# Two heads of a pair in the two column halves of TensorE's array, with the scattering of the second head's rows moved to GpSimd's DMAs

## The chip, the core and the metric

The kernel runs on one core of a Trainium2 chip, in one launch. The metric is the device time of that launch in microseconds. The kernel before took 2098.72 us (median of three runs, 2098.59 to 2098.99).

## What is computed

The reference is a small encoder trunk: two layers, each with a SwiGLU feed-forward block, a mixing block, cross-attention into 256 memory tokens and a second feed-forward block, on 512 frames of 1024 channels, all in float32. The change lies in the mixing block, and there in the gated recurrence of its four heads (128 key channels each):

```python
def step(S, inp):                                # over chunks of 64 frames
    qc, kc, vc, gc = inp                         # gc: log of the gate f
    b = jnp.cumsum(gc, axis=2)
    o_inter = jnp.einsum('bhtk,bhkv->bhtv', qc * jnp.exp(b), S)
    rel = b[:, :, :, None, :] - b[:, :, None, :, :]
    decay = jnp.exp(jnp.where(causal, rel, -jnp.inf))
    A = jnp.einsum('bhtk,bhsk,bhtsk->bhts', qc, kc, decay)
    o = o_inter + jnp.einsum('bhts,bhsv->bhtv', A, vc)
    ...
```

The score of frame t against an earlier frame s is a sum over key channels of q, k and the product of all gates between s and t. The kernel uses chunks of 128 frames in place of 64, and forms the scores without exponentials, by doubling.

## The kernel before

**Layout.** Activations lie transposed, channels on the 128 partitions and 512 frames along the free axis. Most products are made as three single-precision passes of split operands (`mm3`, lines 84 to 86): the weights are cut by ScalarE (line 76) and VectorE (line 77) into a high and a low part, from raw blocks that SyncE's DMAs bring in (line 140). `Weights.next` cuts five blocks and loads seven blocks ahead. Instructions are put in order for each engine by a scheduler, so the order on an engine is near that of the program, but not the same.

**Slots.** Most of the tiles in SBUF come from one pool of 38 equal slots of 4 KB a partition (`s_tile`). A slot is reused when all readers of its tile are done, DMAs that read it among them. Short-lived tiles in PSUM come from a pool of four banks (`ps_tile`), accumulators from another four.

**Score levels.** Heads are held in pairs: `g` is the pair, `hh` the head in it. `qf[g]` and `kg[g]` (128 channels x 2 heads x 512 frames) hold queries and keys times the gates of their own block. At level m (1, 2, 4, ... 64) a block of 2m frames has a first half with keys and a second half with queries, and the scores between the halves are products of `kg` and `qf`. `levels` (line 809) is a generator that is moved on at chosen ticks (`STEPS`), in between the projections that go on at the same time: four gate projections (line 911), the value projection (line 924) and the four projections of the pooling group (line 935).

- Levels 2 to 32 are done by `dense(g, m)` (line 785). For each head and each of the four chunks it multiplies the 64 packed keys (`keys[g]`, copied by `first_halves`, lines 773 and 777) with the 64 query columns of that chunk (line 793): eight float32 products of 64 weight columns and 64 moving columns for a pair, each made by the chip as two passes. Their results, 64 x 64 each, lie side by side in partitions 0 to 63 of one PSUM bank.
- Levels 2 to 16: ScalarE copies the bank to `packed` (line 802, 64 partitions x 512, once for each pair). When both pairs are there, DMAs of ScalarE's queue (line 807) scatter its rows into `spread[m]`, a tile over 128 partitions: 2, 4, 8 and 4 DMAs at levels 2, 4, 8 and 16. One step later `place` (lines 758 to 763) writes the wanted entries into the score tile `atd[g]`, under a mask, on VectorE.
- Level 32: four small copies of ScalarE for each pair (line 798) write straight into `atd[g]`.
- Level 64: line 831, again eight float32 products of 64 x 64 columns for each pair, and one copy for each pair (line 832).
- After the products of a level VectorE multiplies the gates into `kg` (line 849) and `qf` (line 850) for the next one.

After the levels come `turn` (transposes of `kg`, line 874), `carry` (the state, lines 884 to 888) and `read` (the output, lines 974 to 985). Next to them runs the pooling group: `u` (line 939), its running sums on GpSimd (lines 938 and 942), `pt` (line 946), a small product (`pooled`, line 961). GpSimd's own DMAs before the change are adding ones: two sums of weights (line 134) and sums of squares for a norm (line 403).

Of the kernel before, what the change touches and what calls it, by code (L numbers as in the profile page):

```python
# [7 lines left out]
F32 = mybir.dt.float32  # L8
# [6 lines left out]
P = 128  # L15
D = 1024
T = 512
# [3 lines left out]
NT = T // P  # L21
# [25 lines left out]
def trunk_kernel(ctx: ExitStack, tc: tile.TileContext, ap: dict, out: bass.AP):  # L47
    nc = tc.nc
    pe, act, dve, pool = nc.tensor, nc.scalar, nc.vector, nc.gpsimd
# [11 lines left out]
    def ps_tile():  # L61
        return pp.tile([P, 512], F32, tag="ps", name="ps")
# [5 lines left out]
    def s_tile(shape, dt, name):  # L68
        return sp.tile(shape, dt, tag="s", name=name)
# [401 lines left out]
    HT = T // 2  # L471
# [242 lines left out]
    def mix(l, norm, mem, after):  # L714
# [4 lines left out]
        atd = [s_tile([P, 2, NT, P], F32, "atd") for _ in range(2)]  # L719
# [3 lines left out]
        for h in range(H):  # L723
            ps = ps_tile()
# [12 lines left out]
        for h in range(H):  # L737
            ps = ps_tile()
# [6 lines left out]
        def products(a, b):  # L745

            t = tp.tile([P, T], F32, tag="sq", name="qk", bufs=4)
            hl = s_tile([P, 2, T], F32R, "qkp")
            pool.tensor_tensor(t if len(a.shape) == 2 else t.rearrange("p (h n) -> p h n", h=2), a, b, op=ALU.mult)
            split(hl[:, 0], hl[:, 1], t)  # L750
            return hl

        def column_sums(ps, hl):

            for c in range(2):
                pe.matmul(ps, ones_r, hl[:, c], start=c == 0, stop=c == 1)  # L756

        def place(g, m, rows):

            o = atd[g].rearrange("p h i (b e j) -> p (h i) b e j", e=2, j=m)[:, :, :, 1, :]  # L760
            src = rows.rearrange("p (x b j) -> p x b j", x=2 * NT, j=m)
            mk = masks[m].rearrange("p (o b j) -> p o b j", o=1, j=m).broadcast_to([P, 2 * NT, 64 // m, m])
            dve.copy_predicated(o, mk, src)

        keys = [None, None]

        def first_halves(g, m):


            keys[g] = tp.tile([P, T], F32, tag="sq", name="keys", bufs=4)  # L770
            src = kg[g].rearrange("p h (b e j) -> p h b e j", e=2, j=m)[:, :, :, 0, :]
            if m > 4:
                act.copy(keys[g].rearrange("p (h b j) -> p h b j", h=2, j=m), src)
                return
            for hh in range(2):
                dst = keys[g][:, hh * HT:(hh + 1) * HT].rearrange("p (i j b) -> p i b j", i=NT, j=m)
                act.copy(dst, src[:, hh].rearrange("p (i b) j -> p i b j", i=NT))
# [4 lines left out]
        spread = {m: spreads[i % 2] for i, m in enumerate((2, 4, 8, 16))}  # L782
        packed = [None]

        def dense(g, m):


            ps = ps_tile()
            for hh in range(2):
                for i in range(NT):  # L790
                    c = hh * HT + i * 64
                    b = qf[g][:, hh, i * P:(i + 1) * P].rearrange("p (b e j) -> p b e j", e=2, j=m)[:, :, 1, :]
                    pe.matmul(ps[0:64, c:c + 64], keys[g][:, c:c + 64], b, start=True, stop=True)  # L793
            if m == 32:
                for b in range(2):
                    src = ps[b * 32:b * 32 + 32].rearrange("p (h i t) -> p h i t", h=2, i=NT)[:, :, :, b * 32:b * 32 + 32]
                    for hh in range(2):
                        act.copy(atd[g][b * 64:b * 64 + 32, hh, :, b * 64 + 32:b * 64 + 64], src[:, hh])
                return
            if g == 0:  # L800
                packed[0] = s_tile([64, 2, T], F32, "packed")
            act.copy(packed[0][:, g], ps[0:64])
            if g == 1:
                n = max(m, 64 // m)
                for x in range(64 // n):
                    rows = slice(x, P, 2 * m) if m <= 4 else slice(2 * m * x, 2 * m * x + m)
                    nc.scalar.dma_start(spread[m][rows], packed[0][x * n:(x + 1) * n])

        def levels():

            tot = f
            odd = [qf[g].rearrange("p h (n e) -> p h n e", e=2)[:, :, :, 1] for g in range(2)]
            even = [kg[g].rearrange("p h (n e) -> p h n e", e=2)[:, :, :, 0] for g in range(2)]
            near = [[products(q[g][:, hh], kg[g][:, hh]) for hh in range(2)] + [products(odd[g], even[g])] for g in range(2)]
            yield
            for m in (1, 2, 4, 8, 16, 32, 64):
                nb = T // (2 * m)
                tots = [None, None]  # L820
                if 1 < m <= 32:
                    for g in range(2):
                        dense(g, m)
                elif m > 32:
                    for g in range(2):
                        ps = ps_tile()
                        for hh in range(2):
                            for i in range(NT):
                                a = kg[g][:, hh, i * P:i * P + 64]
                                b = qf[g][:, hh, i * P + 64:(i + 1) * P]  # L830
                                pe.matmul(ps[0:64, (hh * NT + i) * 64:(hh * NT + i + 1) * 64], a, b, start=True, stop=True)
                        act.copy(atd[g][0:64, :, :, 64:128].rearrange("p h i t -> p (h i) t"),
                                 ps[0:64, :].rearrange("p (x t) -> p x t", t=64))
                for g in range(2):
                    if m == 1:
                        for hh in range(2):
                            ps = ps_tile()
                            column_sums(ps, near[g][hh])
                            dve.tensor_tensor(atd[g][:, hh], ps.rearrange("p (i t) -> p i t", t=P),
                                              ident.rearrange("p (o t) -> p o t", o=1).broadcast_to([P, NT, P]), op=ALU.mult)  # L840
                            yield
                        ps = ps_tile()
                        column_sums(ps, near[g][2])
                        place(g, m, ps)
                    tv = tot[g].rearrange("p h (b e) -> p h b e", e=2)
                    kv = kg[g].rearrange("p h (b e j) -> p (h b) e j", e=2, j=m)
                    qv = qf[g].rearrange("p h (b e j) -> p (h b) e j", e=2, j=m)
                    tx = tot[g].rearrange("p h (b e) -> p (h b) e", e=2)
                    dve.tensor_tensor(kv[:, :, 0, :], kv[:, :, 0, :], tx[:, :, 1:2].broadcast_to([P, 2 * nb, m]), op=ALU.mult)
                    dve.tensor_tensor(qv[:, :, 1, :], qv[:, :, 1, :], tx[:, :, 0:1].broadcast_to([P, 2 * nb, m]), op=ALU.mult)  # L850
                    nt_ = s_tile([P, 2, nb], F32, "tot") if m == 1 else sm.tile([P, 2, nb], F32, tag=f"tot{m}", name="tot", bufs=2)
                    dve.tensor_tensor(nt_, tv[:, :, :, 0], tv[:, :, :, 1], op=ALU.mult)
                    tots[g] = nt_
                    if m < 32:
                        first_halves(g, 2 * m)
                    if m == 1:
                        yield
                if 2 < m <= 32:
                    for g in range(2):
                        place(g, m // 2, spread[m // 2][:, g])  # L860
                if m > 1:
                    yield
                tot = tots
            last.extend(tot)
# [26 lines left out]
        def recurrent():  # L891
            yield from levels()
            turn(0), turn(1), turn(2)
            yield
# [14 lines left out]
        for h in range(H):  # L909
            ps = ps_tile()  # L910
# [7 lines left out]
        for k2 in range(NK // 2):  # L918
            wh, wl = wts.next()
            for e in range(2):  # L920
                k = 2 * k2 + e
                for i in range(NT):
                    sl = slice(i * P, (i + 1) * P)
                    mm3(accs[i], (norm.h[k][0][:, sl], norm.h[k][1][:, sl]), (wh[:, e], wl[:, e]),
                        start=k == 0, stop=k == NK - 1)
# [6 lines left out]
        for g in POOL_ORDER:  # L932
            win = 2 ** (g + 1)
            ps = ps_tile()
# [5 lines left out]
            src, dst, w_ = u, sa, 1  # L940
            while w_ < win:
                pool.tensor_tensor(dst[:, 16:], src[:, 16:], src[:, 16 - w_:16 + T - w_], op=ALU.add)
                src, dst = dst, (sb if dst is sa else sa)
# [23 lines left out]
        o = [None] * H  # L967
# [328 lines left out]
```

## Time and profile before

| | |
|---|---|
| median of three runs | 2098.72 us |
| the profiled execution: span | 2096.8 us |
| TensorE (PE) busy | 2087.3 us, 100% |
| VectorE (DVE) busy | 1412.3 us, 67% |
| ScalarE (ACT) busy | 919.8 us, 44% |
| GpSimd (POOL) busy | 205.0 us, 10% |
| products of levels 2 to 32 (line 793) | 320 passes |
| products of level 64 (line 831) | 64 passes |
| DMAs of line 807 | 36, on ScalarE's queue |

The page gives no total for the profiled execution beside its span. The span lies 1.9 us below the median of the runs, and that difference is taken as what lies around the span.

The profile names an instruction by engine, line, and "out<-in" tiles. PEld is the loading of weights into TensorE's array, which can go on beside a product; "128*64" is the number of rows and columns of the array that an instruction uses. "x32" is a count of instructions that were merged into one row. The time in square brackets is how long the engine stood idle before a row, and what ended that. A release that the profile can't name is "issue". Queues of an engine are written ACTq, POOLq and SPq.

### The profile page before, as it was taken

Reading aid. Unit: us, or ns where it says so; the run is one execution under the profiler, and the core shown is the slowest. Engines: PE = TensorE matmul, PEld = TensorE weight load, DVE = VectorE, ACT = ScalarE, POOL = GpSimd, SP = SyncE. Lnnn points to the kernel's source line nnn. Section 1 sums busy time; section 2 is a strip of 40 time slices with the busy share of each in tenths; the row PEclk is TensorE's granted clock in tenths of the full one; section 3 lists DMA queues with packets and bytes.
Section 4 is the critical chain, followed back from the end, with each engine's and each line's share of the span. In section 5 each row is a group of like instructions: output and inputs, shape, how many; then the busy total and the mean of one; then the engine's idle time right before and its main releaser. Section 6 shows DMA issues by size and latency. Waiting matters only on the chain.

```text
span 2096.8 us, 29543 instructions
## 1 busy us (share of the span) xinstructions
PE 2087.3 (100%) x11538; PEld 1809.1 (86%) x11538; DVE 1412.3 (67%) x2126; ACT 919.8 (44%) x1465; POOL 205.0 (10%) x204
## 2 busy tenths in 40 slices
PE   9999999999999999999999999999999999999998
PEld 8889898888888888989888898988888888889897
DVE  7758576677646585766776685757776556768575
ACT  6425344434544343544534353445344444435343
POOL 1100000302000110000021000003210001100000
PEclk9999999999999999999999999999999999999999
DMA  5364554233533246646425746532334331474552
GB/s 187 119 182 124 145 156 161 61 99 98 151 103 103 61 131 171 157 122 185 123 69 153 188 116 177 158 108 71 92 112 135 111 112 45 141 208 124 146 138 79
DMA packets 107868, 268.33 MB, mean 128 GB/s; under 512 B 10832, under 2 KB 12880, under 8 KB 107728
## 3 DMA queue, kind: packets, MB, share of 16 engines
q1 hardware_dynamic: 93952, 224.49, 32.9%
q0 software_dynamic: 11952, 38.02, 10.3%
q10 hardware_dynamic: 1824, 3.93, 0.8%
q8 instruction: 91, 1.49, 0.3%
q14 instruction: 49, 0.40, 0.1%
HBM read 256.70 MB, written 2.10 MB: 123 GB/s over the span
## 4 chain that ended last, share of the span: by engine, by line
PE 98%; DVE 1%; issue 1%; ACT 0%; POOL 0%; POOLq 0%; ACTq 0%; DVEq 0%
PE ps L86 19%; PE ps L84 19%; PE ps L85 19%; PE acc L554 8%; PE acc L84 8%; PE acc L85 8%; PE acc L86 8%; PE acc L555 4%; PE ps L1025 1%; PE ps L793 1%; PE ps L1026 1%; PE ps L974 0%; PE ps L1091 0%; PE acc L346 0%; PE ps L756 0%
## 5 line engine op out<-in xcount | busy, mean ns | idle before, releaser
L77 DVE TENSOR_TENSOR wlo<-raw,whi 128x1024 fp32r<-128x1024 f32 (+1 forms) x334 | 394.5, 1202 | 78.4 <-ACT whi L76 63.2
L76 ACT CAST whi<-raw 128x1024 fp32r<-128x1024 f32 (+1 forms) x334 | 330.3, 1018 | 113.1 <-DMA raw<-in_ffn_w_dram 49.9
L85 PE MATMUL ps<-h,whi 128*128 128x512 f32 x848 | 330.2, 390 | 0.0
L84 PE MATMUL ps<-h,whi 128*128 128x512 f32 x848 | 329.7, 391 | 0.0
L86 PE MATMUL ps<-h,wlo 128*128 128x512 f32 x848 | 329.5, 390 | 0.0
L554 PE MATMUL acc<-bhl,whi 128*128 128x512 f32 x744 | 266.3, 398 | 0.0
L86 PE MATMUL ps<-bhl,wlo 128*128 128x256 f32 x744 | 210.8, 284 | 0.2
L85 PE MATMUL ps<-bhl,whi 128*128 128x256 f32 x744 | 209.9, 283 | 0.0
L84 PE MATMUL ps<-bhl,whi 128*128 128x256 f32 x744 | 209.8, 283 | 0.0
L555 PE MATMUL acc<-bhl,wlo 128*128 128x256 f32 x744 | 204.8, 281 | 0.0
L76 ACT CAST whi<-wsum 128x1024 fp32r<-128x1024 f32 x124 | 130.1, 1050 | 151.8 <-DVE wsum L165 87.3
L86 PEld LDWEIGHTS ps<-h,wlo 128*128 128x128 f32 x848 | 159.2, 188 | 33.4
L84 PEld LDWEIGHTS ps<-h,whi 128*128 128x128 f32 x848 | 159.1, 188 | 33.1
L85 PEld LDWEIGHTS ps<-h,whi 128*128 128x128 f32 x848 | 159.2, 188 | 32.9
L77 DVE TENSOR_TENSOR wlo<-wsum,whi 128x1024 fp32r<-128x1024 f32 x124 | 153.8, 1240 | 47.7 <-ACT whi L76 45.5
L554 PEld LDWEIGHTS acc<-bhl,whi 128*128 128x128 f32 x744 | 137.7, 189 | 24.0
L84 PEld LDWEIGHTS ps<-bhl,whi 128*128 128x128 f32 x744 | 141.6, 190 | 4.1
L86 PEld LDWEIGHTS ps<-bhl,wlo 128*128 128x128 f32 x744 | 141.5, 190 | 2.5 <-DVE wlo L77 1.6
L555 PEld LDWEIGHTS acc<-bhl,wlo 128*128 128x128 f32 x744 | 141.1, 190 | 2.8
L85 PEld LDWEIGHTS ps<-bhl,whi 128*128 128x128 f32 x744 | 141.6, 190 | 1.9
L134 POOL DMA_DIRECT2D wsum<-in_ffn_w_dram x62 | 53.9, 869 | 765.5 <-DMA wsum<-in_ffn_w_dram 364.5
L84 PE MATMUL acc<-ahl,whi 128*128 128x512 f32 x328 | 128.0, 390 | 0.0
(271 smaller groups left out, 4128.9 us busy)
## 6 DMA issues: line engine op xcount, KB each, us to landing
raw<-in_ffn_w_dram SPq DMA_DIRECT2D x198, 512.0 KB
wsum<-in_ffn_w_dram SPq DMA_DIRECT2D x124, 256.0 KB
wsum<-in_ffn_w_dram POOLq DMA_DIRECT2D x62, 512.0 KB, 6.8
raw<-in_w_in_dram SPq DMA_DIRECT2D x32, 512.0 KB
raw<-in_ffn_w_dram SPq DMA_DIRECT2D x62, 256.0 KB
raw<-in_w_out_dram SPq DMA_DIRECT2D x16, 512.0 KB
raw<-in_xa_wk_dram SPq DMA_DIRECT2D x16, 512.0 KB
raw<-in_xa_wq_dram SPq DMA_DIRECT2D x16, 512.0 KB
```

Of the source, the lines that this page charges most:

```text
L76: act.copy(hi, src)
L77: dve.tensor_tensor(lo, src, hi.bitcast(F32), op=ALU.subtract)
L84: pe.matmul(o, a[0], b[0], start=start, stop=False, skip_group_check=more)
L85: pe.matmul(o, a[0], b[1], start=False, stop=False, skip_group_check=more)
L86: pe.matmul(o, a[1], b[0], start=False, stop=stop, skip_group_check=more)
L134: nc.gpsimd.dma_start(s1, c2, accum_op=ALU.add)
L554: pe.matmul(ps.rearrange("p (c t) -> p c t", t=HT), w[0], t, start=start and k == 0, stop=False, skip_group_check=True)
L555: pe.matmul(ps[:, :HT], w[1], t[:, 0], start=False, stop=k == 3, skip_group_check=True)
L793: pe.matmul(ps[0:64, c:c + 64], keys[g][:, c:c + 64], b, start=True, stop=True)
L1025: pe.matmul(ps.rearrange("p (c m) -> p c m", m=M), whl[0][:, k], mn[k], start=k == 0, stop=False, skip_group_check=True)
L1026: pe.matmul(ps[:, :M], whl[1][:, k], mn[k][:, 0], start=False, stop=k == NK - 1, skip_group_check=True)
```

## The change

In `dense` both pairs of a level now share one PSUM bank. The first head (`hh` 0) is written to partitions 0 to 63 and the second to partitions 64 to 127, that is, its 64 columns lie in the other half of the array; the pair `g` picks the half of the bank's 512 columns. The loop runs over chunks outside and heads inside, so that consecutive products alternate between the two halves of the array. Level 64 does the same, with a bank for each pair.

The copy to SBUF is then one of 128 x 512 for both pairs, in place of two of 64 x 512. The scattering DMAs are made for each head: those of the first head on ScalarE's queue, as many as before with half the bytes, those of the second head on GpSimd's queue, 18 in each layer that were not there before. Level 32 has as many small copies as before, from other partitions. Level 64 has two copies for each pair in place of one.

```diff
-            ps = ps_tile()
-            for hh in range(2):
-                for i in range(NT):
+            if g == 0:
+                packed[0] = ps_tile()
+            ps = packed[0]
+            for i in range(NT):
+                for hh in range(2):
                     c = hh * HT + i * 64
                     b = qf[g][:, hh, i * P:(i + 1) * P].rearrange("p (b e j) -> p b e j", e=2, j=m)[:, :, 1, :]
-                    pe.matmul(ps[0:64, c:c + 64], keys[g][:, c:c + 64], b, start=True, stop=True)
+                    o = g * HT + i * 64
+                    pe.matmul(ps[hh * 64:hh * 64 + 64, o:o + 64], keys[g][:, c:c + 64], b, start=True, stop=True)
             if m == 32:
-                for b in range(2):
-                    src = ps[b * 32:b * 32 + 32].rearrange("p (h i t) -> p h i t", h=2, i=NT)[:, :, :, b * 32:b * 32 + 32]
-                    for hh in range(2):
-                        act.copy(atd[g][b * 64:b * 64 + 32, hh, :, b * 64 + 32:b * 64 + 64], src[:, hh])
+                for hh in range(2):
+                    for b in range(2):
+                        src = ps[hh * 64 + b * 32:hh * 64 + b * 32 + 32, g * HT:(g + 1) * HT]
+                        src = src.rearrange("p (i t) -> p i t", i=NT)[:, :, b * 32:b * 32 + 32]
+                        act.copy(atd[g][b * 64:b * 64 + 32, hh, :, b * 64 + 32:b * 64 + 64], src)
                 return
-            if g == 0:
-                packed[0] = s_tile([64, 2, T], F32, "packed")
-            act.copy(packed[0][:, g], ps[0:64])
             if g == 1:
+                t = s_tile([P, 2, HT], F32, "packed")
+                act.copy(t.rearrange("p g t -> p (g t)"), ps)
                 n = max(m, 64 // m)
                 for x in range(64 // n):
                     rows = slice(x, P, 2 * m) if m <= 4 else slice(2 * m * x, 2 * m * x + m)
-                    nc.scalar.dma_start(spread[m][rows], packed[0][x * n:(x + 1) * n])
+                    for hh in range(2):
+                        queue = nc.gpsimd if hh else nc.scalar
+                        queue.dma_start(spread[m][rows, :, hh * HT:(hh + 1) * HT], t[hh * 64 + x * n:hh * 64 + (x + 1) * n])
...
                     for g in range(2):
                         ps = ps_tile()
-                        for hh in range(2):
-                            for i in range(NT):
+                        for i in range(NT):
+                            for hh in range(2):
                                 a = kg[g][:, hh, i * P:i * P + 64]
                                 b = qf[g][:, hh, i * P + 64:(i + 1) * P]
-                                pe.matmul(ps[0:64, (hh * NT + i) * 64:(hh * NT + i + 1) * 64], a, b, start=True, stop=True)
-                        act.copy(atd[g][0:64, :, :, 64:128].rearrange("p h i t -> p (h i) t"),
-                                 ps[0:64, :].rearrange("p (x t) -> p x t", t=64))
+                                pe.matmul(ps[hh * 64:hh * 64 + 64, i * 64:(i + 1) * 64], a, b, start=True, stop=True)
+                        for hh in range(2):
+                            act.copy(atd[g][0:64, hh, :, 64:128], ps[hh * 64:hh * 64 + 64, :HT].rearrange("p (i t) -> p i t", t=64))
```

## The prediction, made before the changed kernel ran

> **What bounds the kernel now.** I read the page first (busy time, then the chain that ended last), then the timeline of TensorE around one score level, then the chain and the waits behind the levels, in both layers.
>
> ```profile
> span 2096.8 us, 29543 instructions
> PE 2087.3 (100%) x11538; PEld 1809.1 (86%) x11538; DVE 1412.3 (67%) x2126; ACT 919.8 (44%) x1465; POOL 205.0 (10%) x204
> PE 98%; DVE 1%; issue 1%; ACT 0%; POOL 0%; POOLq 0%; ACTq 0%; DVEq 0%
> ```
>
> TensorE is busy throughout and is 98% of the chain. A microsecond taken from TensorE is a microsecond of the end, unless another engine is close behind at that place; work moved between the others is free as long as TensorE doesn't come to wait for it. So two questions decide: how long TensorE takes for a level, and who is close behind.
>
> Level 2 in layer 0, on TensorE, its weight loads, and their single durations:
>
> ```profile
> 425.54 0.39 PE L86 MATMUL ps<-h,wlo 128*128 128x512 f32 x1
> 425.85 2.08 PE L793 MATMUL ps<-qf,keys 128*64 128x64 f32 x32
> 427.86 0.50 PE L84 MATMUL ps<-h,whi 128*128 128x512 f32 x1
> 428.20 0.39 PE L85 MATMUL ps<-h,whi 128*128 128x512 f32 x1
> 428.43 0.39 PE L86 MATMUL ps<-h,wlo 128*128 128x512 f32 x1
> ...
> 425.85 1.94 PEld L793 LDWEIGHTS ps<-qf,keys 128*64 128x64 f32 x32 [0.35 <-issue]
> ...
> L793 PEld LDWEIGHTS ps<-qf,keys x320: 132/138/138, 425.9 to 1500.9; 128*64 128x64 f32 x160
> ```
>
> Products overlap, so I count from start to start. An ordinary product of 512 columns takes 428.43 - 428.20 = 0.23 us. From 425.54 to 428.20 lie 2.66 us with two ordinary products in them: the 32 passes of the level (two pairs, 16 each) cost 2.66 - 0.46 = 2.20 us. The loads spread over 1.94 us, of which the last alone is 138 ns: (1.94 - 0.138) / 31 = 58 ns a pass, 1.86 us for 32. The other 0.34 us are the two switches between 128 and 64 columns (a first start 0.31 us after the last ordinary one, and 0.34 us after the first ordinary one, in place of 0.23). With 320 passes of line 793 and 64 of line 831 there are 12 such groups: 12 x 2.20 = 26.4 us, 1.3% of the time. That is all that this change can work on in TensorE.
>
> **The change part by part.**
>
> *The two halves of the array.* The number of passes stays. What may go is their distance: if one half loads and multiplies while the other does, two passes take the 58 ns of one. No row of before has two products in different halves, so the price has to be bounded. Above: 58 ns a pass as now, no gain. Below: half, 16 x 58 ns = 0.93 us less for each group, 12 x 0.93 = 11.2 us in all. (Halving also the switches, 12 x 0.17 more, isn't possible: they stay.) A neighbouring row says what sets the 58 ns:
>
> ```profile
> 28.66 0.94 PE L346 MATMUL acc<-ones,sq 128*128 128x1 f32 x8
> 29.47 0.49 PE L86 MATMUL ps<-h,wlo 128*128 128x512 f32 x1
> ```
>
> Eight passes that move one column each, but load 128, take (29.47 - 28.66) / 8 = 101 ns. So small products go at the pace of the loading of weights, nearly twice as long for twice the columns. The question is then whether the loads of the two halves can lie beside each other. I take that they do, by the nearest row there is: in the ordinary stream a load runs beside a product on the same rows.
>
> ```profile
> 428.66 0.40 PE L84 MATMUL ps<-h,whi 128*128 128x512 f32 x1
> 428.66 0.19 PEld L85 LDWEIGHTS ps<-h,whi 128*128 128x128 f32 x1
> ```
>
> The load of L85 starts with the product of L84, so loads are taken ahead of what follows; with separate columns the same freedom can reach past a waiting product of the other half. It is a choice, not a proof, and the first rival is its opposite.
>
> The Trainium skill, TensorEngine Tiling (Array Packing), section Tiling Modes, says that different tiles can load weights and multiply in parallel, and that only a change of the mode drains the array; that would give the 11.2 us. Against it, TensorE: Matmul & The Clock Gate, section on packing small matmuls, says that a load overlaps with products in flight only where the group of rows differs, which is not so here. The two rows just shown disagree with that as it stands, since their rows are the same 128.
>
> *Level 32 in one bank.* The second pair now writes the bank from which four copies read the first pair's scores, so it has to wait for them and comes as a group of its own.
>
> ```profile
> 461.14 1.77 ACT L798 COPY atd<-ps 32x128 f32<-32x128 f32 x8 [0.64 <-PE ps L793]
> ```
>
> Two more switches for each layer, 2 x 0.34 = 0.7 us. If nothing ordinary is put between the pairs, TensorE also waits for half of the 1.77 us, some 2 us over both layers; there are ordinary products ready at that place, so I take nothing, and keep the 2 us for the range.
>
> *Level 64 and what is late next.* Behind the levels another chain is close. The chain that ended last, in layer 0 and then in layer 1, with TensorE's wait:
>
> ```profile
> 460.02 2.01 PE ps L793 x32
> ...
> 464.88 0.57 DVE qf L850
> ...
> 470.67 0.93 DVE kg L849
> ...
> 481.08 1.50 POOL sa L942
> ...
> 488.25 0.71 PE ps L974 x4
> 1499.12 2.01 PE ps L793 x32
> 1508.15 2.01 PE ps L831 x32
> ...
> PE ps L974 <- DVE st L888: 0.4, 1, 0.4
> ```
>
> In layer 0 the chain leaves TensorE after level 32 and runs over VectorE and GpSimd to 488.25; level 64 isn't in it. What levels 2 to 32 save moves this chain forward too, since it starts at TensorE, but what level 64 saves there (0.9 us) is lost again as a wait. In layer 1 both levels are in the chain and count in full.
>
> *Copies.* Four times per layer one copy of 128 x 512 replaces two of 64 x 512 (0.58 us each); ScalarE gains some 0.5 us each time, level 64 gives a part of that back with two half copies for one. ScalarE is 44% busy and hardly in the chain: nothing either way.
>
> *DMAs.* ScalarE issues as many as before with half the bytes. GpSimd gets 18 in each layer. No row shows a plain one on its queue; the nearest are adding ones of GpSimd, and ScalarE's scattering ones:
>
> ```profile
> L403 POOL DMA_DIRECT2D far<-sq x21: 850/864/928, 346.2 to 1724.5; - x21
> DMA to landing us min/median/max: 3.2/3.6/6.0
> L807 ACTq DMA_DIRECT2D spread<-packed x36: 518/626/1212, 429.6 to 1494.6; - x36
> ...
> 458.27 0.11 POOL L938 MEMSET u<- 128x16 f32 x1 [50.43 <-DMA spread<-packed]
> ```
>
> Bounds: 0.52 us an issue (ScalarE's shortest) to 1.21 (its longest), landing 0.9 us after the last issue (ScalarE's last issue began at 456.2 and `u` was free at 458.27) to 6.0. I take 0.86 and 3.6, the same engine's medians. 18 x 0.86 = 15.5 us fall in a hole of 50.43 us in which GpSimd waits, so its engine time is free. Behind them on its queue are the memset of `u` and the pooling sums. What counts is who waits for the rows: VectorE's `place`, and behind it on its engine the eviction of `v`, cuts of weights and `u`.
>
> ```profile
> 446.38 0.58 ACT L802 COPY packed<-ps 64x512 f32<-64x512 f32 x1
> ...
> 458.08 1.33 DVE L763 COPY_PREDICATED atd<-fixed,spread 128x512 f32<-128x512 int32 x2 [3.40 <-DMA spread<-packed]
> ...
> 1485.48 0.58 ACT L802 COPY packed<-ps 64x512 f32<-64x512 f32 x1
> ...
> 1493.69 1.31 DVE L763 COPY_PREDICATED atd<-fixed,spread 128x512 f32<-128x512 int32 x2
> ...
> 1508.02 1.46 DVE L77 TENSOR_TENSOR wlo<-raw,whi 128x1024 fp32r<-128x1024 f32 x1 [4.40 <-issue]
> ```
>
> Level 8 has most: eight DMAs, 8 x 0.86 + 3.6 = 10.5 us after the copy's end. Layer 0: 446.96 + 10.5 = 457.5, before the place at 458.08. Layer 1: 1486.06 + 10.5 = 1496.6, 2.9 us after the place at 1493.69; VectorE has 4.40 us idle a little later, and the weights are cut five blocks ahead, each worth 24 products of 0.23 us. I cost it at nothing; without that cover it is the third rival.
>
> **Sum**, against the profiled execution's own 2096.8 us of span, which is 1.9 us under the median of 2098.7: - 11.2 (overlap) + 0.7 (level 32) + 0.9 (level 64 in layer 0) = - 9.6 us, a span of 2087.2, and with the same 1.9 us around it 2089.1 us.
>
> **Rivals.**
>
> *The loads take turns.* If one path feeds both halves, the loads still come 58 ns apart, and as the row of line 346 says that loads set the pace, nothing is gained. For it speaks that row, and the order of the program: each float32 product is two passes, so a half has two loads in a row before the other half's turn. Against it only the freedom shown above. Time: 2098.7 + 0.7 = 2099.4.
>
> The Trainium skill gives a reason for it in TensorE: Matmul & The Clock Gate, section Weight-path perf modes: fast loads read weights 32 bits at a time, "no win fp32". A float32 load of 128 rows would then already fill that width, and two could not lie beside each other. No run here shows it yet.
>
> *A change of half drains.* If going to the other half costs what a switch of width costs, 0.34 / 2 = 0.17 us, each of the 16 products of a group pays it: 16 x 0.17 = 2.7 us, times 12 = 33 us, 2098.7 + 33 = 2131. This would be slower; it decides from the point where a change of half costs over 58 ns. Against it: both halves have the same width, and the 58 ns run evenly from product to product with new weights each time.
>
> *GpSimd's rows come late.*
>
> ```profile
> L134 POOL DMA_DIRECT2D wsum<-in_ffn_w_dram x62: 853/862/1053, 104.7 to 2011.1; - x62
> 468.92 1.23 DVE L77 TENSOR_TENSOR wlo<-raw,whi 128x1024 fp32r<-128x1024 f32 x1 [2.26 <-issue]
> ```
>
> At an issue of 1.05 us (the longest of line 134, GpSimd's other DMA) and a landing of 6.0, level 8 needs 14.4 us: 3.3 us late in layer 0 and 6.8 in layer 1, and `u` and the pooling chain move by as much, in front of the place where TensorE waits already. VectorE's idle time takes up to 2.3 and 4.4 us of it back. That is + 3.4 to + 10.1; I take the middle, 6.7, which without overlap gives 2099.4 + 6.7 = 2106.1. It decides from about 3 us of delay on. Against it: the medians, by which it is hidden.
>
> **How the numbers follow.** Overlap 0.48, loads in turn 0.36, late rows without overlap 0.11, draining 0.05. The forecast is 2089.1. Its own range goes from 2086.5 (level 64 in layer 0 not lost, level 32 not split, and loads a little closer than 58 ns) to 2094 (partial overlap, TensorE waiting at level 32). About 0.2%, 4.2 us, can be told from no change. The whole range takes in the loads in turn and the smaller half of the late rows: 2086.5 to 2103.5. Faster 0.48, same 0.36, slower 0.16 (late rows and draining).
>
> **What would show it.** In the changed profile: line 793's 32 passes in about 1.1 us from first start to the next ordinary product, in place of 2.01, is right; 2.0 is the first rival; over 3 is the second. Level 32 shows as two groups. Line 807's GpSimd issues near 0.86 us, and VectorE's wait at line 763 not over some 3 us. TensorE's waits between level 64 and `read` grow by about 1 us in layer 0 and not in layer 1. The prediction is wrong if the passes keep their distance, or if they close up and the time is given back as waits of TensorE in that place.

## The result, and the profile after

The changed kernel takes **2092.61 us** (median of seven runs, 2092.24 to 2093.02) against 2098.72 (seven runs, 2098.20 to 2099.38): 6.1 us less, a ratio of 0.997 with a 95% interval of 0.996 to 0.9981. The forecast was 2089.1 in a range of 2086.5 to 2103.5. So its sign and its mechanism were right, and 3.5 of the 9.6 us that it promised didn't come.

The page of the changed kernel:

```profile
span 2090.7 us, 29622 instructions
PE 2077.4 (99%) x11538; PEld 1798.0 (86%) x11538; DVE 1408.4 (67%) x2126; ACT 918.0 (44%) x1461; POOL 230.3 (11%) x240
```

TensorE is busy 9.9 us less, but the span is only 6.1 us shorter. That difference is the first thing to see: TensorE was given what was promised, and something gave part of it back. The timeline of TensorE around level 2 in layer 0, and its weight loads there (line 796 is what line 793 was):

```profile
425.60 0.39 PE L86 MATMUL ps<-h,wlo 128*128 128x512 f32 x1
425.91 1.16 PE L796 MATMUL ps<-qf,keys 128*64 128x64 f32 x32
427.00 0.50 PE L84 MATMUL ps<-h,whi 128*128 128x512 f32 x1
427.33 0.40 PE L85 MATMUL ps<-h,whi 128*128 128x512 f32 x1
...
425.91 1.02 PEld L796 LDWEIGHTS ps<-qf,keys 128*64 128x64 f32 x32 [0.35 <-issue]
```

The same 32 passes, counted as before: 427.33 - 425.60 = 1.73 us, less two ordinary products, 1.27 us in place of 2.20. The loads fill 1.02 us in place of 1.94, though each still lasts 138 ns. The two switches of width (0.31 us before the group, 0.33 us after it) are as they were. So the passes of the two halves lie wholly beside each other, 0.93 us less a group.

Levels 32 and 64 in layer 0, the later rows of the same timeline:

```profile
456.33 0.69 PE L796 MATMUL ps<-qf,keys 128*64 128x64 f32 x16
...
462.38 0.69 PE L796 MATMUL ps<-qf,keys 128*64 128x64 f32 x16
...
464.81 1.15 PE L836 MATMUL ps<-qf,kg 128*64 128x64 f32 x32
```

Level 32 has come apart into two groups, 6 us from each other, with an ordinary projection between them.

To see where time comes and goes I set the starts of the same instructions of TensorE in the two profiled executions beside each other (all in us from the start of the span; the difference is after less before):

| first product of | before | after | difference |
|---|---|---|---|
| level 2, layer 0 | 425.85 | 425.91 | + 0.06 |
| level 4 | 432.85 | 432.01 | - 0.85 |
| level 8 | 443.25 | 441.47 | - 1.77 |
| level 16 | 450.92 | 448.22 | - 2.70 |
| level 32 | 459.95 | 456.33 | - 3.63 |
| level 64 | 468.99 | 464.81 | - 4.18 |
| turn (transposes) | 477.93 | 472.83 | - 5.11 |
| read, layer 0 | 488.25 | 483.69 | - 4.55 |
| level 2, layer 1 | 1464.95 | 1460.37 | - 4.58 |
| level 64, layer 1 | 1508.09 | 1499.25 | - 8.84 |
| turn, layer 1 | 1517.03 | 1507.27 | - 9.76 |
| read, layer 1 | 1526.32 | 1517.78 | - 8.54 |
| last product of all | 2089.09 | 2080.62 | - 8.47 |
| end of the span | 2096.78 | 2090.70 | - 6.08 |

Each level gains 0.91 to 0.93 us, level 32 only 0.55, level 64 again 0.93. Between `turn` and `read` 0.56 us are lost in layer 0 and 1.22 in layer 1. After the last product, where nothing of the change runs, 2.4 us more are lost: from the start of that product to the end it takes 10.08 us in place of 7.69.

TensorE's waits (who waited for whom, us in total, times, longest):

```profile
PE ps L879 <- DVE u L944: 1.1, 2, 0.7
...
PE ps L979 <- DVE st L893: 0.8, 2, 0.4
PE ps L889 <- DVE st L893: 0.4, 2, 0.2
```

These are the waits between `turn` and `read`. The last 2.4 us are in the closing instructions of the program, which the page doesn't count as busy. One of them, in every engine's list, is named DRAIN. GpSimd's and SyncE's, first in the kernel before, then after (duration in ns, least, median and most, then first and last start):

```profile
L1292 SPq DRAIN  x3: 7/7/7, 2095.4 to 2096.3; - x3
L1292 POOLq DRAIN  x3: 40/93/5285, 2090.7 to 2096.5; - x3
```

```profile
L1297 SPq DRAIN  x3: 7/7/7, 2086.9 to 2090.2; - x3
L1297 POOLq DRAIN  x3: 46/97/7656, 2082.3 to 2090.4; - x3
```

In the changed kernel the last output lands at 2086.42, and SyncE comes to its DRAIN at 2086.93. GpSimd's long one starts when its last instruction is issued. Before, it ended at 2090.7 + 5.3 = 2096.0, 0.6 us after SyncE was through. After, it ends at 2082.3 + 7.7 = 2090.0, 3.0 us after SyncE, and the last steps of all engines follow it. The 36 DMAs that GpSimd issues more have made it 2.37 us longer, long after they landed; the experiments on this DRAIN, below, test that.

GpSimd's DMAs themselves (issue in ns, then time to landing):

```profile
L812 POOL DMA_DIRECT2D spread<-packed x36: 501/557/632, 428.1 to 1486.3; - x36
...
DMA to landing us min/median/max: 1.8/2.5/4.5
```

They are cheaper than I took them, 0.56 us in place of 0.86, and land after 2.5 us in place of 3.6. VectorE waits for scattered rows 6.8 us in all, where it was 8.0.

### The profile page after: what moved, and what is told of

It is laid out like the page before. It is cut to its first block, busy times and chain, and to the rows that moved or that the text cites. A ratio compares the mean times of both kernels' runs of the same rounds, so it can differ in the third digit from the quotient of the medians.

```text
span 2090.7 us, 29622 instructions
## 1 busy us (share of the span) xinstructions
PE 2077.4 (99%) x11538; PEld 1798.0 (86%) x11538; DVE 1408.4 (67%) x2126; ACT 918.0 (44%) x1461; POOL 230.3 (11%) x240
## 4 chain that ended last, share of the span: by engine, by line
PE 97%; DVE 2%; issue 1%; POOL 0%; ACT 0%; POOLq 0%; DVEq 0%; ACTq 0%
PE ps L86 19%; PE ps L84 19%; PE ps L85 18%; PE acc L554 8%; PE acc L84 8%; PE acc L85 8%; PE acc L86 8%; PE acc L555 4%; PE ps L1030 1%; PE ps L1031 1%; PE ps L796 1%; DVE wlo L77 0%; PE ps L979 0%; PE ps L1096 0%; PE acc L346 0%
```

## The experiments

Times are medians of timed runs beside the kernel before on the same chip; that took 2098.7 to 2098.8 each time. The runs of one kernel spread over 0.8 to 3.1 us, so what is smaller than a microsecond is read from the starts in the traces.

### Does the order matter, or only the halves?

```diff
-            for i in range(NT):
-                for hh in range(2):
+            for hh in range(2):
+                for i in range(NT):
```

The same in level 64.

> The changed kernel, with the loop over heads outside the loop over chunks: eight passes in one half of the array, then eight in the other, same numbers of everything. Theory (passes overlap only when neighbours in the order lie in different halves): 58 ns a pass again except at the borders, a group of 32 in about 1.8 to 1.9 us, the time about 2100 to 2103. Rival (TensorE looks far enough ahead to pair passes that are eight apart): 1.1 us a group and 2092.6.

2095.72 us, and neither theory. Its timeline at level 2:

```profile
425.60 1.56 PE L796 MATMUL ps<-qf,keys 128*64 128x64 f32 x32
```

A group gains 0.54 us in place of 0.93 (from level 4 on the first product of the next level is 0.54 us further ahead each time). The starts of the first passes of that group, in ns from the first one, as the trace has them:

```
0 110 168 226 285 291 343 401 402 460 461 519
```

In the kernel before, the passes of a group, all in one half, start 57 to 60 ns apart (106 to 110 for the first step), so I take 285 and 291 to be of different halves. In the program the second half's first pass is the ninth. By this reading TensorE has taken it ahead of three passes of the first half that stand before it. It looks some passes ahead, not eight, and so it finds a partner for a part of them only. Alternating heads in the loop is what gives the full overlap. The page of the Trainium skill that I weighed in the prediction (TensorE: Matmul & The Clock Gate, section on packing small matmuls) says that products start and end strictly in the order of the program; this row doesn't agree.

### What is lost between the transposes and read

**Level 32's bank.**

```diff
-            if g == 0:
+            if g == 0 or m == 32:
                 packed[0] = ps_tile()
```

> The changed kernel, with a bank of its own for the second pair at level 32. Theory (the shared bank makes the second pair wait for four copies, an ordinary projection slips in between, and VectorE's chain of gate products behind the second pair starts late, so that read waits): one group of 32 passes at level 32, two switches less for each layer (0.37 us each layer), and the loss between the transposes and read (0.55 us in layer 0, 1.22 in layer 1) gone for the most part: about 2090.1 us. Rival (the loss before read comes from VectorE and GpSimd being the slower chain there whatever level 32 does): only the switches, about 2091.9. Rival (those switches are hidden too, as that stage isn't bound by TensorE): 2092.6.

2092.32 us lies between the last two theories of the three. The trace is for the last: the final product of all comes only 0.15 us earlier than in the changed kernel. Level 32 is one group again (1.15 us for 32 passes at 456.73), and in layer 1 it gains the full 0.93 us, so the 0.37 us of switches were real. But `read` in layer 1 starts 8.62 us earlier than before, where it was 8.54: the rest is given back. The wait has only moved to another product:

```profile
PE ps L84 <- DVE u L944: 2.6, 2, 1.7
```

So my theory that the late second pair was to blame fell.

**Level 64 in one half, as before.**

> The changed kernel, with level 64 in one half of the array as in the kernel before. Theory (what level 64 saves is given back before read, since VectorE's chain is later there): the 0.93 us of each layer come back in TensorE's work before the transposes, the wait before read shrinks by as much, time unchanged at 2092.6, within 0.4. Rival (level 64 counts in full): 2 x 0.93 more, 2094.5. As it was predicted (lost in layer 0, full in layer 1): 2093.5.

2092.18 us, 0.4 less than the changed kernel, with ranges that overlap; nothing is lost without it. `turn` is 4.24 us ahead in layer 0 and 8.81 in layer 1, one level less, and `read` is 4.51 and 8.76 ahead, no less than in the changed kernel. What level 64 saves is worth nothing in either layer. The prediction had it lost in layer 0 alone.

**Without the masked writes of level 16** (the score tile then lacks level 16):

```diff
-                if 2 < m <= 32:
+                if 2 < m <= 16:
```

> The changed kernel without the masked writes of level 16's scores into the score tile (two for each layer, left out). Theory (VectorE's chain from level 32 to read sets the start of read): one of them is in that chain with 1.65 us, so read starts up to 0.55 us earlier in layer 0 and 1.2 in layer 1, about 2091 us. Rival (GpSimd's running sums are as late): unchanged, 2092.6.

2091.54 us; the last product comes 0.94 us earlier than in the changed kernel. VectorE's work counts there, for about half of the 1.75 us that the theory allowed.

**Without six of the ten running sums of each layer's pooling** (each group then has only its first sum):

```diff
-            while w_ < win:
+            while w_ < 2:
```

> The changed kernel with one running sum in each pooling group; the other six of each layer are left out. Theory (GpSimd's sums, and VectorE beside them at 1.45 us in place of 0.68, are what is late before read): the loss between transposes and read goes, 0.55 us in layer 0 and 1.22 in layer 1: about 2090.8 us. Rival (VectorE's chain is late without them too): 2092.6, or less than half of that gain.

2089.59 us, and no wait of TensorE is left there at all. The last product is 2.9 us earlier, more than the 1.8 that were lost. From the start of `turn` to that of `read` it now takes 9.30 us in both layers; the changed kernel takes 10.87 and 10.51, the kernel before 10.32 and 9.29. So layer 0 had lost 1.0 us there before the change already. The stretch before `read` is held by GpSimd's sums together with VectorE, which goes slower beside them; how much belongs to either, this run doesn't separate. The changed kernel's chain that ended last, there in layer 1, shows both:

```profile
1498.65 1.65 DVE atd L763
...
1501.45 1.45 DVE kg L854
1502.90 1.45 DVE qf L855
1504.34 1.99 DVE wlo L77
...
1510.68 1.43 POOL sa L947
1512.17 1.05 POOL sb L947
...
1515.58 1.03 DVE pthl L77
...
1517.78 0.71 PE ps L979 x4
```

The gate products of lines 854 and 855 take 0.68 us where none of GpSimd's sums runs (the second pair's in layer 0, at 472.16 and 472.76) and 1.45 us in this chain.

### Whose queue carries the second head's rows

**SyncE's:**

```diff
-                        queue = nc.gpsimd if hh else nc.scalar
+                        queue = nc.sync if hh else nc.scalar
```

> The changed kernel, with the second head's DMAs on SyncE's queue in place of GpSimd's. Theory (the 36 GpSimd DMAs cost 2.37 us at the end through GpSimd's closing DRAIN): DRAIN back at 5.3 us, the end 2.4 us nearer to the last product; if the rest stays as it is, 2090.2 us. Rival (the place of the DMAs matters more): SyncE waits in order for the copies, its weight loads behind them come late, TensorE waits for cuts of weights: 2092.6 or more.

2094.31 us (median of ten runs). GpSimd's closing DRAIN is back at 5285 ns, and the end comes 7.69 us after the start of the last product, as in the kernel before. But the last product comes 3.4 us later than in the changed kernel, more than that gave, and the loss is around level 64:

```profile
PE ps L836 <- DVE qf L855: 5.4, 2, 2.7
```

TensorE waits 2.7 us in each layer for VectorE's gate products ahead of level 64. Both parts of the expectation came true, the rival's by another wait than it named. What makes those gate products late was not followed further.

**ScalarE's, all 36 + 36** (`queue = nc.scalar`):

> The changed kernel, with the second head's DMAs on ScalarE's queue too. Theory of the DRAIN: 5.3 us again, 2.4 us nearer. ScalarE then issues 16 DMAs of 0.70 us at level 8, 11 us in a row in place of 5.1, and level 16's copy waits behind them. If that is hidden: 2090.2 us. Rival: rows and cuts are 5 to 6 us late at levels 8 and 16 and VectorE's chain before read with them, 2 to 5 us for each layer: 2094 to 2100.

2109.42 us, ratio 1.0052 (1.0039 to 1.0064), slower than the kernel before. ScalarE's timeline at level 8, and TensorE's wait ahead of level 64:

```profile
444.84 11.57 ACTq L812 DMA_DIRECT2D spread<-packed  x15
456.45 0.58 ACT L806 COPY packed<-ps 128x512 f32<-128x512 f32 x1 [11.50 <-DMA spread<-packed]
...
PE ps L836 <- DVE qf L855: 17.9, 2, 9.3
```

Issues block the engine that makes them: level 16's copy waits 11.5 us behind them. After it VectorE's gate products come late, and TensorE waits about 9 us for them in each layer. The prediction's third rival, rows that come late, can be seen at work here, on another queue. Spreading the second head's rows by GpSimd is worth 2109.4 - 2092.6 = 16.8 us against that, the longer closing DRAIN included.

### GpSimd's closing DRAIN

**The kernel before with its 36 DMAs on GpSimd's queue:**

```diff
-                    nc.scalar.dma_start(spread[m][rows], packed[0][x * n:(x + 1) * n])
+                    nc.gpsimd.dma_start(spread[m][rows], packed[0][x * n:(x + 1) * n])
```

> The kernel before, with all 36 scattering DMAs of line 807 on GpSimd's queue and nothing else changed. Theory (GpSimd's closing DRAIN takes about 64 ns for each DMA that GpSimd issued: 5.285 us for 83 before, 7.656 us for 119 in the changed kernel): 119 DMAs, so a closing DRAIN of 7.6 to 7.7 us, the end 2.4 us later after the last product than in the kernel before, about 2101.1 us. Rival (it goes by rows or bytes moved, not by DMAs): the rows are the same 4 KB each and half as many pieces as in the changed kernel, so the DRAIN is near 6.5 us and the time near 2099.9. Rival (the DRAIN has nothing to do with these DMAs): 5.3 us and 2098.7.

2100.28 us, a ratio of 1.0007 (0.9998 to 1.0016), so the time alone doesn't settle it. The trace does:

```profile
L1292 POOLq DRAIN  x3: 46/98/7607, 2090.6 to 2098.7; - x3
```

7.61 us with rows of 4 KB, 7.66 with twice as many pieces of 1 KB in the changed kernel: half the bytes in twice the pieces make 0.05 us of difference. The span of the profiled execution is 2.2 us longer while the last product comes 0.1 us earlier.

**The norms' sums of squares on VectorE alone** (`far=0`, 21 adding DMAs fewer):

> The changed kernel with the sums of squares for the norms added on VectorE alone (far=0): 21 adding DMAs of GpSimd fewer, 98 in all. Theory of 64 ns a DMA: closing DRAIN 6.3 us in place of 7.66, the end 1.35 us nearer: about 2091.3 us if VectorE's 21 further additions of 0.69 us are hidden. Rival (only the DMAs of line 812 count in the DRAIN): DRAIN 7.66 and 2092.6.

2091.82 us (2090.5 to 2093.5), with a DRAIN of another length than expected:

```profile
L1297 POOLq DRAIN  x3: 46/98/5328, 2083.0 to 2088.8; - x3
```

98 DMAs give 5.33 us, and 83 gave 5.29. So the price isn't 64 ns for each, as I had read it from two points. If the parts simply add, the 36 scattering ones cost 66 ns each, the 21 sums of squares 111 and the 62 sums of weights 48. A step of some 2.3 us somewhere between 98 and 119 DMAs would fit the four durations as well. What sets it is open. VectorE's additions cost TensorE 0.7 us.

**The last inverse root taken from GpSimd**, so that its DRAIN can start earlier:

```diff
-            pool.tensor_tensor(col, v, nhalf[:, 0:1], op=ALU.pow)
+            if ahead:
+                act.activation(col, v, AF.Sqrt)
+                dve.reciprocal(col, col)
+            else:
+                pool.tensor_tensor(col, v, nhalf[:, 0:1], op=ALU.pow)
+            if i == 2:
+                warm = sm.tile([P, 1], F32, tag="warm", name="warm", bufs=1)
+                act.activation(warm, v, AF.Sqrt)
```

> The changed kernel; only the last tile's inverse root at the very end is taken from GpSimd (a root on ScalarE and a reciprocal on VectorE, with a root earlier so that its table is there). Theory (GpSimd's closing DRAIN takes 64 ns for each of its 119 DMAs and starts when GpSimd's last instruction is done): it starts near 2075 instead of 2082, takes 7.7 us and ends before SyncE's last output has landed, so the end comes 2.4 us nearer to the last product: about 2090.2 us, up to 0.3 more for the two instructions in place of one. Rival (the DRAIN waits for the end of the others, or for the last DMAs): the end stays 2.97 us behind SyncE's, 2092.6 us.

2089.36 us, 3.25 us less than the changed kernel, with the last product at the very same time:

```profile
L1304 SPq DRAIN  x3: 7/7/7, 2086.7 to 2087.0; - x3
L1304 POOLq DRAIN  x3: 46/98/7661, 2074.5 to 2087.3; - x3
```

The DRAIN is as long as ever, but runs from 2074.5 to 2082.1, most of it beside TensorE's last products, and is through before SyncE. So the end does wait for this DRAIN where it comes last.

**The same edit in the kernel before:**

> The kernel before with the same edit of the last inverse root. Theory: there the closing DRAIN (83 DMAs, 5.3 us) ended 0.6 us after SyncE's, which is no more than the order of the closing steps, so nothing is gained: 2098.7, within 0.4. Rival (the edit itself makes the end shorter, DRAIN or not): about 2 us less here too, 2096.5.

2097.93 us: 0.8 us less, more than the 0.4 I allowed, and far from the rival's two. The ratio's interval (0.9987 to 1.0004) doesn't exclude no change, but the traces agree: from the start of the last product to the end it takes 6.93 us in place of 7.69 here, and 6.95 in place of 10.08 in the changed kernel. With the edit both kernels close alike. A part of the 0.8 us, 0.6 us, is the lag that GpSimd's DRAIN had there too. So of the 3.25 us about 2.4 belong to the change.

### A version that beats both

With the last root on ScalarE, and the four pooling projections ahead of the value projection (in the order of the weights too), so that the running sums lie beside the levels and not behind them.

> The kernel with the last root on ScalarE, and with the four pooling projections ahead of the value projection, so that GpSimd's running sums lie 22 us earlier beside the levels. Theory (what is late before read is the stretch in which GpSimd's sums, and VectorE's gate products beside them at 1.45 us in place of 0.68, come behind level 32): the loss of 0.55 and 1.22 us before read goes, TensorE's last product comes 1.8 to 3 us earlier, 2086.4 to 2087.6 us. Rival (VectorE's own chain is as late, or sums hold up GpSimd's scattering DMAs, which come behind them in its queue): 2089.4 or more.

**2088.06 us** (2087.8 to 2088.62), a ratio to the kernel before of 0.995 (0.9936 to 0.9963). The last root alone gave 2089.36; the new order gives the other 1.3 us. The last product comes 10.0 us earlier than before in place of 8.5; that is 1.5 us more, and the theory's lower bound, 1.8 us, isn't quite met. TensorE's waits before `read` have shrunk to this:

```profile
PE ps L979 <- DVE h L80: 0.4, 2, 0.2
```

## Why the prediction was right in sign and a third too large

- **Two halves, 11.2 us:** right: 0.91 to 0.93 us for each of 12 groups, 11.1 in all. That the loads, which set the pace, lie beside each other was the choice on which all hung; one row of another shape had been its ground, and the prediction gave it 0.48. It came true, but was not derived. That the order of the loop matters, as the experiment on it shows, was not in the prediction. The first rival (loads take turns) and the second (a change of half drains) are refuted by the timeline of level 2. The Trainium skill's rule in TensorE: Matmul & The Clock Gate, section on packing small matmuls, by which a load overlaps with products only where the group of rows differs, is not borne out by the 1.02 us of loads on the same rows; what TensorEngine Tiling (Array Packing), section Tiling Modes, says of tiles that load and multiply in parallel is.
- **Level 32 in one bank, + 0.7 us:** right in kind and size, 0.37 us in each layer, and TensorE doesn't wait, since 23 ordinary products go between the pairs. It is of no consequence at the end, as the experiment with a bank of its own shows.
- **Level 64 and what is late next, + 0.9 us:** the mechanism was right, the term too small. It costs 0.56 us in layer 0 and 1.22 in layer 1, 1.8 us together. The step that failed is "In layer 1 both levels are in the chain and count in full": the other chain was near there too, and once TensorE was ahead by a few microseconds it became the later one. In layer 0 the prediction saw a wait of 0.4 us, where 1.0 us was lost already. A chain shows who was last, not by how much.
- **Copies, nothing:** nothing is seen of them.
- **DMAs, hidden:** right for the levels; issue and landing were overestimated (0.86 and 3.6 us for 0.56 and 2.5), and the third rival didn't come.
- **The sum:** the step that failed most. It has no term for the end of the program: what TensorE gains was taken to reach the end in full. The 1.9 us around the span did stay the same (2092.6 - 2090.7), but inside it 2.4 us were added between the last product and the end, by a closing DRAIN that no view of busy time shows. "Its engine time is free" was right for the issue of those DMAs and wrong for what they leave behind.
- **The range:** its upper end, 2103.5, doesn't come out of the prices given. From 2099.4, late rows at + 3.4 to + 6.7 would reach 2102.8 to 2106.1. The result lies well below, so nothing hung on it.

Together: - 11.1 + 0.7 + 1.8 + 2.4 = - 6.2 us, and 6.1 were measured, in span and in the median.

## What to carry to other kernels

Small products whose weights fill half the array's columns were had here in pairs at the price of one, with neighbours in the program in different halves (0.93 us less for 32 passes); with eight passes of one half ahead of eight of the other it was 0.54. So interleave them. Before counting a saving on the busiest engine in full, work out how late the second chain is at that place, not only whether it is in the chain that ended last. And look at the program's closing instructions: work put on an idle queue was paid there.

## What the runs showed of the hardware

- Two streams of float32 passes on the same 128 rows and different halves of columns run side by side without loss: their starts come in pairs, most of them 6 or 7 ns apart, and 58 ns from pair to pair.
- A product in the other half of the array can overtake earlier ones: in the version with heads outside the sixth start, 6 ns after the fifth, can hardly be other than the ninth pass of the program.
- GpSimd's closing DRAIN took 5.29, 5.33, 7.61 and 7.66 us with 83, 98, 119 and 119 DMAs. It started with GpSimd's last instruction: at 2082.3 it held up the end, at 2074.5 it didn't.
